# One hybrid encoder layer on one core: the feed-forward norm by way of memory, and the second stage's products and merges in another order

## The chip, the cores and the metric

The kernel runs on one core of one Trainium2 chip. The metric is the time of one execution in microseconds of device time (us). A core has five engines that work side by side and wait for each other through semaphores: PE (TensorE, matrix products; PEld is its loading of weights), DVE (VectorE), ACT (ScalarE), POOL (GpSimd) and SP (SyncE, which here only issues DMA transfers). Each engine takes its instructions strictly in the order of its own queue, so an instruction that waits holds back all that stand behind it.

## What is computed

One layer over 1024 frames of width 1024, in float32:

```python
u = rms_norm(h, mix_norm_gain)
proj = u @ w_in                  # attention and delta-rule inputs
o_att = band attention of 8 heads;  o_dn = gated delta rule of 4 heads
h = h + concat([rms_norm(o_att), o_dn]) @ w_out
z = rms_norm(h, ffn_norm_gain) @ w_ff1        # 1024 -> 4096
h = h + square(relu(z)) @ w_ff2               # 4096 -> 1024
```

The change concerns the first instructions, the step `h + ... @ w_out`, and the two feed-forward products.

## The kernel before

Activations lie transposed: features on the 128 partitions, frames along the free axis, in two halves of 512 frames. A float32 product is made of three fp32r matmuls: each operand is split into a high part (a cast, mostly on ACT) and a low part (operand minus high part, mostly on DVE), in `split`, and the products high·high, low·high and high·low are summed. A tile name ends in `_h` or `_l` accordingly.

The order of the instructions on each engine is made at compile time by a scheduler from the order of the code; nothing is reordered while it runs. `tc.issue_after(x)` asks it to place what follows behind the instruction `x`.

**Start.** For each of eight blocks k the kernel loads 128 rows of `w_in` (tile `wdk_r`, by `load_w`) and a block of x (tile `xt`, by `load_xt`), splits the weights (`wdk_h`, `wdk_l`), scales x by the norm's gain `mgain` (`uh` on ACT, `ul` on DVE) and squares it (`xs`). The first product of the kernel, `dk_ps` at L299, needs `uh` and `wdk_h` of block 0.

**Output projection (`out_proj`).** It makes h in four quarters, `rows(j, hf)`: j is the half of the features and hf the half of the frames. Each quarter is four 128x512 results `op`; after each, DVE adds x (L948, tile `h`), ACT squares it (L954) and POOL adds the square to the sum `op_q` (L955). Each quarter of h goes to memory (`h_dr`, L956), and after that ACT multiplies it by the gain of the second norm (L958). After both quarters of a half, `norm(hf, acc)` sums over partitions with a float32 matmul by a matrix of ones (tile `hs`, L963), takes 1/(mean+eps) with two DVE instructions (L964, L965) and writes that to memory (`r2_dr`, L966). `ff1` reads it back as `r2`. Since relu(r·z)² is r²·relu(z)², the norm's factor is applied after the square (`emit`, L1057).

**First feed-forward product (`ff1`).** Eight blocks of 512 columns of `w_ff1`. In each block a 2x2 blocking of the product is done with seven products instead of eight, `q1` to `q7`, whose operands are quarters or sums of quarters of the weights (`wa`, `ws`) and of h (`b11`, `b21`, `t1`, `t2`, `b22`, `t3`, `t4`; these are made once, by `uop`, in place in the quarters of h, and kept). A product is 24 matmuls of 128x512 into one of four PSUM buffers. Blocks 0 and 1 are interleaved at first: q1 of both, q2 of both, then the rest of each block. The results go to memory as `f_dr`.

**Second feed-forward product (`ff2`).** Four blocks of 1024 rows of `w_ff2`, again seven products `p1` to `p7` of 48 matmuls each, into two PSUM buffers. In block 0 the results of p1, p5, p6 and p7 are copied to `y` by ACT, the others are added by DVE. Block 3 (`last`) also merges the seven sums into the four quarters of the output and stores them; `p4` comes last, one PSUM buffer after the other, and is subtracted and stored in four pieces (L1252, L1253).

## Time and profile before

| | |
|---|---|
| time, median of 3 runs | 1311.7 us (1311.33 to 1311.72) |
| the profiled execution | 1309.98 us, of it the span 1307.9 us |
| busy: PE, DVE, ACT, POOL | 1265.2, 936.2, 553.0, 301.8 us |
| mean granted clock of TensorE | 0.988 of full speed |
| `out_proj` ends, `ff1` starts | about 673 us |
| `ff2` starts | about 990 us |
| last matmul starts | 1300.6 us |

The span is the time from the first to the last record of the profile. A busy share of 97% for PE says that nearly every microsecond of the span has a matmul in flight; it doesn't say at which clock. All times below are from the span's start.

### The profile page before, as it was taken

The page shows a single profiled execution, that of the slowest core. Times are in us where ns is not written, and L with a number is a line of the kernel's source. Part 1 is how long each engine was busy: PE and PEld are TensorE (multiplying, and loading weights), DVE is VectorE, ACT ScalarE, POOL GpSimd, SP SyncE. Part 2 cuts the span into 40 slices and gives each one's busy share as a digit, 9 for nine tenths or more (in the row PEclk, how much of TensorE's full clock was granted, in tenths as well). Part 3 has the DMA queues.
Part 4 walks back from the last instruction along what each step waited for, and adds up shares of the span by engine and source line. Part 5 has one row for each costly group of instructions (what it writes and reads, how often), then busy time and mean ns, then how long its engine had stood idle before and what let it go on. Part 6 is the DMA issues. An engine that isn't in the chain of part 4 may idle for free.

```text
span 1307.9 us, 17991 instructions
## 1 busy us (share of the span) xinstructions
PE 1265.2 (97%) x6658; PEld 1041.5 (80%) x6658; DVE 936.2 (72%) x1395; ACT 553.0 (42%) x918; POOL 301.8 (23%) x507
## 2 busy tenths in 40 slices
PE   8999999999999998979998999999998999999997
PEld 6778878788888777858776888888887888888886
DVE  7899978554056565853639756776669897897997
ACT  7233232233266563754335444444456443333330
POOL 4426552543033364533310000000000000000034
PEclk9999999999999999989998999999999999999999
DMA  7214254665573532114341323323379523322002
GB/s 219 70 45 142 94 157 123 137 161 155 193 225 111 153 94 74 56 46 165 117 153 61 111 100 121 104 92 102 109 249 353 169 86 113 129 82 97 15 33 96
DMA packets 129255, 160.63 MB, mean 123 GB/s; under 512 B 22800, under 2 KB 71952, under 8 KB 128656
## 3 DMA queue, kind: packets, MB, share of 16 engines
q1 hardware_dynamic: 111760, 138.51, 34.1%
q10 hardware_dynamic: 17408, 20.98, 4.7%
q8 instruction: 52, 0.85, 0.3%
q14 instruction: 35, 0.29, 0.1%
HBM read 111.75 MB, written 47.71 MB: 122 GB/s over the span
## 4 chain that ended last, share of the span: by engine, by line
PE 82%; DVE 10%; DMA 3%; issue 2%; POOL 1%; ACT 1%; POOLq 1%; SPq 0%; ACTq 0%; DVEq 0%
PE q L1051 21%; PE p L1128 20%; PE op L163 5%; PE av_ps L163 3%; PE aq_ps L163 3%; PE dk_ps L299 3%; PE t_o L851 3%; PE g_ps L163 3%; PE ak_ps L163 2%; PE dv_ps L163 2%; PE dq_ps L163 2%; PE t_tpb L830 1%; PE t_tpa L841 1%; PE t_sb L778 1%; DMA t_q<-q_dr 1%
## 5 line engine op out<-in xcount | busy, mean ns | idle before, releaser
L1197 POOL TENSOR_TENSOR y<-y,y 128x1024 f32<-128x1024 f32 x6 | 19.4, 3250 | 600.5 <-DVE y L1193 581.6
L794 DVE CUSTOM_DVE_ANT_0 t_pb<-t_sb,biasn 128x256 f32<-128x256 f32 (+1 forms) x64 | 25.7, 403 | 56.8 <-PE t_sb L779 31.2
L1193 DVE TENSOR_TENSOR y<-y,p 128x1024 f32<-128x1024 f32 x46 | 55.3, 1219 | 6.3 <-PE p L1128 5.4
L163 PE MATMUL op<-mh,wo_h 128*128 128x512 f32 x128 | 50.3, 393 | 0.6 <-ACT wo_h L142 0.3
L163 PE MATMUL op<-ml,wo_h 128*128 128x512 f32 x128 | 50.5, 394 | 0.0
L163 PE MATMUL op<-mh,wo_l 128*128 128x512 f32 x128 | 48.3, 391 | 0.0
L809 ACT ACTIVATE t_pb<-t_pb,t_nm 128x256 f32<-128x256 f32 (+1 forms) x64 | 31.7, 495 | 23.1 <-DVE t_nm L803 15.0
L948 DVE TENSOR_TENSOR h<-op,op_x 128x512 f32<-128x512 f32 x16 | 10.8, 688 | 29.7 <-PE op L163 29.7
L851 PE MATMUL t_o<-t_ta,vt 128*64 128x128 f32 x240 | 29.7, 299 | 1.8 <-DVE t_ta L844 1.1
L955 POOL TENSOR_TENSOR op_q<-op_q 128x512 f32<-128x512 f32 x14 | 19.6, 1399 | 48.2 <-ACT op_q L954 48.0
L803 DVE CUSTOM_DVE_ANT_0 t_pa<-t_sa,biaso,t_nm 128x384 f32<-128x384 f32 (+2 forms) x48 | 26.3, 549 | 5.5 <-PE t_sa L779 3.3
L163 PEld LDWEIGHTS op<-mh,wo_h 128*128 128x128 f32 x128 | 24.0, 188 | 6.8 <-ACT wo_h L142 0.7
L163 PEld LDWEIGHTS op<-mh,wo_l 128*128 128x128 f32 x128 | 24.0, 188 | 5.4 <-issue 0.4
L163 PEld LDWEIGHTS op<-ml,wo_h 128*128 128x128 f32 x128 | 24.0, 188 | 5.1 <-issue 0.2
L299 PE MATMUL dk_ps<-uh,wdk_h 128*128 128x512 f32 x56 | 21.7, 413 | 5.5 <-ACT uh L180 5.5
L778 PE MATMUL t_sb<-ks,t_q 128*128 128x256 f32 (+1 forms) x72 | 23.2, 333 | 3.7 <-DMA t_q<-q_dr 3.7
L812 ACT ACTIVATE t_pa<-t_pa,t_nm 128x384 f32<-128x384 f32 (+2 forms) x48 | 26.5, 552 | 0.1
L841 PE MATMUL t_tpa<-ident,t_pa 128*128 128x128 f32 x120 | 21.9, 288 | 4.5 <-ACT t_on L879 3.3
L163 PE MATMUL g_ps<-uh,wg_l 128*128 128x512 f32 x64 | 25.3, 398 | 0.5 <-POOL wg_l L145 0.5
L163 PE MATMUL dv_ps<-ul,wdv_h 128*128 128x512 f32 x64 | 25.5, 398 | 0.0
L851 PEld LDWEIGHTS t_o<-t_ta,vt 128*64 128x64 f32 x240 | 17.9, 143 | 9.5 <-issue 1.9
L163 PE MATMUL dq_ps<-uh,wdq_h 128*128 128x512 f32 x64 | 25.4, 396 | 0.0
(1101 smaller groups left out, 4429.7 us busy)
## 6 DMA issues: line engine op xcount, KB each, us to landing
wa<-in_w_ff_dram SPq DMA_DIRECT2D x32, 512.0 KB
a<-in_w_ff_dram SPq DMA_DIRECT2D x32, 512.0 KB
b<-f_dr SPq DMA_DIRECT2D x32, 512.0 KB
t_q<-q_dr SPq DMA_DIRECT2D x32, 256.0 KB
f_dr<-yy ACTq DMA_DIRECT2D x16, 512.0 KB
f_dr<-zz ACTq DMA_DIRECT2D x12, 512.0 KB
xt<-in_x_t_dram SPq DMA_DIRECT2D x16, 256.0 KB
ks<-k_dr SPq DMA_DIRECT2D x16, 256.0 KB
```

Of the source, the lines that this page charges most:

```text
L163: nc.tensor.matmul(ps, a, b, start=(i == 0), stop=(i == n - 1))
L299: nc.tensor.matmul(ps[ct], a[:, s], b, start=(k + m == 0), stop=(k == NKT - 1 and m == 2))
L778: nc.tensor.matmul(o, q[:, i * P:(i + 1) * P], k[:, c], start=True, stop=False)
L794: nc.vector.tensor_tensor_reduce(sb[:, c], bk[:, c], new[g][pp][:, c], -1.0, 3.0e38, ALU.add, ALU.min, nm[:, 4 + i:5 + i])
L803: nc.vector.tensor_tensor_reduce(sa[e][:, 0:wa], bk[:, 0:wa], old[g][i][:, 384 - wa:384], -1.0, nm[:, 4 + i:5 + i], ALU.add, ALU.min, nm[: ...
L809: nc.scalar.activation(sb[:, c], sb[:, c], AF.Exp, bias=m, scale=-1.0, accum_out=T["sums"][:, 4 + i:5 + i])
L812: nc.scalar.activation(sa[e][:, 0:wa], sa[e][:, 0:wa], AF.Exp, bias=m, scale=-1.0, accum_out=T["sums"][:, i:i + 1])
L841: nc.tensor.transpose(tp[:, js], sa[e][:, js], ident)
L851: nc.tensor.matmul(po[64 * e:64 * e + 64, pp * P:(pp + 1) * P], vt[k0 + j][:, 64 * h:64 * h + 64], (ta[e] if j < na else tb)[:, c:c + P], ...
L1051: nc.tensor.matmul(part(ps, q), l[:, s], r, start=(k + m == 0), stop=(k == 3 and m == 2))
L1128: nc.tensor.matmul(part(ps[q // 2], q % 2), l[:, s], part(r, k), start=(i + k + m == 0), stop=(i + k + m == 4))
L1193: nc.vector.tensor_tensor(y[i][m], y[i][m], ps[m], op)
```

## The change

1. At the start the matrix of ones is made first, and eight float32 128x128 matmuls on it, whose result nobody reads, are put at the head of PE's queue. The first block of x is loaded from ACT's queue instead of SP's, and on SP `mgain` comes first and the weights of block 0 after it.
2. `norm` is gone. `out_proj` writes the two sums of squares to memory (`sq_dr`), and `ff1` reads both back as one tile `acc`. `norm_col`, called when q1 of blocks 0 and 1 is issued, sums over partitions with eight float32 matmuls of one column each (`hcol`) and takes 1/(mean+eps) of a 128x8 tile (`r_col`). `norm_row`, called after the q2s, spreads it with eight float32 128x128 matmuls (`hrow`), and ACT copies the result to `r2`.
3. `square` (relu and square) is taken out of `emit` and comes ahead of it. In blocks 0 and 1 the generator yields between the two.
4. `LAST` orders the splits of the operands b22, t3 and t4 behind the first split of t1, t2 and b22.
5. `ff2` makes its products in the order p1, p2, p5, p3, p6, p7, p4 instead of p1, p5, p2, p3, p6, p7, p4, with the loads in step.
6. In the last block `y6 += y1` moves from DVE to POOL and comes early, `y7 += y6` and `y3 += y6` come before p6 is added, and p6 and p7 are then added straight to the outputs (y3 and y7; y4 and y5). Two of the last four stores go to ACT's queue.

```diff
+WARM = 8
+LAST = {"b22": "t1", "t3": "t2", "t4": "b22"}
...
+    ones = cpool.tile([P, P], F32, name="ones")
+    nc.gpsimd.memset(ones, 1.0)
+    warm = bank(ps_o, "warm")
+    for i in range(WARM):
+        nc.tensor.matmul(warm[:, 0:P], ones, ones, start=True, stop=True)
     ident = cpool.tile([P, P], F32, name="ident")
...
-        nc.sync.dma_start(out=raw, in_=x_t[k, :, hf * TH:(hf + 1) * TH])
         if not hf and not k:
+            nc.scalar.dma_start(out=raw, in_=x_t[0, :, 0:TH])
             nc.sync.dma_start(out=mgain, in_=mix_gain)
+        else:
+            nc.sync.dma_start(out=raw, in_=x_t[k, :, hf * TH:(hf + 1) * TH])
...
     for k in range(NKT):
-        w_dk.append(load_w(w_in[k * P:(k + 1) * P, DK:DK + 512], f"wdk_{k}"))
+        if k:
+            w_dk.append(load_w(w_in[k * P:(k + 1) * P, DK:DK + 512], f"wdk_{k}"))
         load_xt(0, k)
+        if not k:
+            w_dk.append(load_w(w_in[0:P, DK:DK + 512], "wdk_0"))
...
         acc = rows(1, 0, acc)
-        norm(0, acc)
+        nc.sync.dma_start(out=sq_dr[:, 0:TH], in_=acc)
         mixed(1)
         acc = rows(1, 1, None)
         acc = rows(0, 1, acc)
-        norm(1, acc)
+        nc.sync.dma_start(out=sq_dr[:, TH:SEQ], in_=acc)
...
+        def norm_col():
+
+            acc = page2("ut4", "acc")
+            nc.sync.dma_start(out=acc, in_=sq_dr)
+            ps = psw.tile([P, 1024], F32, tag="bk", name="hcol")
+            for q in range(NT):
+                nc.tensor.matmul(ps[:, q:q + 1], acc[:, q * P:(q + 1) * P], ones[:, 0:1], start=True, stop=True)
+            nc.vector.tensor_scalar(r_col, ps[:, 0:NT], 1.0 / DM, EPS, ALU.mult, ALU.add)
+            nc.vector.reciprocal(r_col, r_col)
+
+        def norm_row():
+
+            ps = psw.tile([P, 1024], F32, tag="bk", name="hrow")
+            for q in range(NT):
+                nc.tensor.matmul(ps[:, q * P:(q + 1) * P], r_col[:, q:q + 1].broadcast_to([P, P]), ident,
+                                 start=True, stop=True)
+            nc.scalar.copy(r2.rearrange("p a t -> p (a t)"), ps)
...
-                bop = uop(key)
+                ah, al = parts(src, n + "a", key)
+                if key in LAST:
+                    hi, lo = begun[LAST[key]]
+                    with tc.issue_after(hi), tc.issue_after(lo):
+                        bop = uop(key)
+                else:
+                    bop = uop(key)
...
-        for _ in range(2):
+        for i in range(2):
             for g in first:
                 next(g)
+            (norm_row if i else norm_col)()
...
             accumulate(1, product(f"p1{kb}", lambda i: (a11[i], b11[i])))
-            accumulate(5, product(f"p5{kb}", prep5))
             accumulate(2, product(f"p2{kb}", lambda i: (a12[i], b21[i])))
             if last:
                 merge(nc.gpsimd, 2, 1)
                 store(y[2], 0, 0)
-            accumulate(3, product(f"p3{kb}", prep3))
-            accumulate(6, product(f"p6{kb}", prep6))
+                merge(nc.gpsimd, 6, 1)
+            accumulate(5, product(f"p5{kb}", prep5))
             if last:
-                merge(nc.vector, 6, 1)
                 merge(nc.gpsimd, 3, 5)
                 for m in range(2):
                     nc.gpsimd.tensor_tensor(y[5][m], y[5][m], h11[m], ALU.add)
-                merge(nc.vector, 3, 6)
-                store(y[3], 0, 1)
-            accumulate(7, product(f"p7{kb}", prep7))
+            accumulate(3, product(f"p3{kb}", prep3))
+            ps = product(f"p6{kb}", prep6)
             if last:
                 merge(nc.vector, 7, 6)
+                merge(nc.vector, 3, 6)
+                accumulate(3, ps)
+                store(y[3], 0, 1)
+                accumulate(7, ps)
+                merge(nc.vector, 4, 7)
                 merge(nc.gpsimd, 5, 7)
-                merge(nc.vector, 4, 7)
+            else:
+                accumulate(6, ps)
+            ps = product(f"p7{kb}", prep7)
+            if last:
+                accumulate(4, ps)
+                accumulate(5, ps)
                 store(y[5], 1, 1)
+            else:
+                accumulate(7, ps)
...
-                nc.sync.dma_start(out=out[0, (4 + q) * P:(5 + q) * P, 0:TH], in_=t)
+                (nc.scalar if q % 2 else nc.sync).dma_start(out=out[0, (4 + q) * P:(5 + q) * P, 0:TH], in_=t)
```

What the scheduler makes of it is seen at three places. In the rows, a number behind a name tells apart tiles of one name. First, ACT's queue at the start of the program, before:

```order
L142 ACT_TABLE_LOAD
L142 CAST wdk_h<-wdk_r 128x512
L185 ACTIVATE xs_176<-xt_171 128x512
L180 ACTIVATE uh_0_141<-xt_171,mgain 128x512
L142 CAST wdk_h<-wdk_r 128x512
L180 ACTIVATE uh_1_143<-xt_184,mgain 128x512
```

and now:

```order
L179 DMA xt_174<-in_x_t_dram 128x512
L184 ACT_TABLE_LOAD
L184 ACTIVATE uh_0_150<-xt_174,mgain 128x512
L189 ACTIVATE xs_179<-xt_174 128x512
L146 CAST wdk_h<-wdk_r 128x512 x2
L184 ACTIVATE uh_1_152<-xt_193,mgain 128x512
L189 ACTIVATE xs_197<-xt_193 128x512
```

The load of ACT's function table stood ahead of all waits and now stands behind the x transfer, in front of the first instruction that reads `mgain`; the cast of the first weights has moved from the first to the third place.

Second, DVE's queue at the start of `ff1`. Before, from the two instructions of `norm(1, acc)` on (`op_q` is the sum of squares, the `h` are quarters of h that become t1 and t3 in place, `t1h`/`t1l` their parts):

```order
L964 TENSOR_SCALAR op_q<-hs_7328 128x512
L145 TENSOR_TENSOR b22l_7650<-h_7069,b22h_7649 128x1024
L965 RECIPROCAL op_q<-op_q 128x512
L145 TENSOR_TENSOR b22l_7654<-h_7069,b22h_7653 128x1024
L1018 TENSOR_TENSOR h_6731<-h_7198,h_6731 128x1024 x2
L1075 TENSOR_TENSOR ws_0_7559<-wa_0_7555,wa_0_7557 128x1024
L1018 TENSOR_TENSOR h_7198<-h_7069,h_7198 128x1024 x2
L145 TENSOR_TENSOR t1l_7568<-h_6731,t1h_7567 128x1024
```

and now, from the low part of t1 up to the reciprocal of the norm:

```order
L147 TENSOR_TENSOR t1l_7589<-h_6740,t1h_7588 128x1024
L147 TENSOR_TENSOR q_0a_l<-ws_0_7580,q_0a_h 128x1024
L147 TENSOR_TENSOR b22l_7671<-h_7074,b22h_7670 128x1024
L1018 TENSOR_TENSOR h_6740<-h_7074,h_6740 128x1024
L147 TENSOR_TENSOR t1l_7594<-h_6740,t1h_7593 128x1024
L1104 TENSOR_TENSOR ws_0_7580<-ws_0_7580,wa_0_7399 128x1024
L147 TENSOR_TENSOR b22l_7675<-h_7074,b22h_7674 128x1024
L1032 TENSOR_SCALAR r_col<-hcol 128x8
L147 TENSOR_TENSOR t2l_7630<-h_6740,t2h_7629 128x1024
L1018 TENSOR_TENSOR h_6740<-h_7074,h_6740 128x1024
L1108 TENSOR_TENSOR wa_0_7401<-wa_0_7401,ws_0_7580 128x1024
L1033 RECIPROCAL r_col<-r_col 128x8
```

The reciprocal of 128x512 has gone; that of 128x8 stands eleven rows further on than this piece begins, behind the low parts of t1, q5 and b22 and the subtractions that make t2.

Third, ACT's queue where `ff2` starts (the y copies take the results of p1, the `p50` and `p20` tiles are operands of p5 and p2 in block 0). Before:

```order
L1191 COPY y_9450<-p_9496 128x1024
L142 CAST p50b_h<-b_0_9462 128x1024
L142 CAST p50a_h<-s_0_9601 128x1024
L1191 COPY y_9450<-p_9497 128x1024
L142 CAST p50b_h<-b_0_9464 128x1024
L142 CAST p20a_h<-a_0_9478 128x1024
L1058 DMA f_dr<-yy_9174 128x2x512
L142 CAST p20b_h<-b_0_9482 128x1024
```

and now:

```order
L1221 COPY y_9473<-p_9519 128x1024
L146 CAST p50b_h<-b_0_9485 128x1024
L146 CAST p50a_h<-s_0_9692 128x1024
L1221 COPY y_9473<-p_9520 128x1024
L146 CAST p50b_h<-b_0_9487 128x1024
L1083 DMA f_dr<-yy_9197 128x2x512
L146 CAST p20a_h<-a_0_9489 128x1024
L146 CAST p20b_h<-b_0_9493 128x1024
```

The casts of the operands of p2 still stand behind the copies and the casts for p5, while on PE the first two matmuls of p2, which read `p20a_h` and `p20b_h`, now stand directly behind p1 and ahead of all of p5.

## Rows read from the trace of the kernel before

**Rows 1.** The page: busy time, share of the span and instructions of PE and of its weight loads.

```profile
PE 1265.2 (97%) x6658; PEld 1041.5 (80%) x6658; DVE 936.2 (72%) x1395; ACT 553.0 (42%) x918; POOL 301.8 (23%) x507
```

**Rows 2.** Waits of PE over the whole span: what it waited for, us in total, how often, the longest.

```profile
PE dk_ps L299 <- ACT uh L180: 5.5, 1, 5.5
PE hs L963 <- POOL op_q L955: 2.9, 1, 2.9
PE p L1128 <- DVE p50b_l L145: 2.9, 1, 2.9
PE q L1051 <- DVE z L1057: 2.9, 1, 2.9
```

**Rows 3.** Windows: from:to in us, its length, then for each engine the busy us and the number of instructions, the granted clock of PE (1.00 is full speed, 0.50 half), the share of the DMA engines and GB/s.

```profile
498.00:499.00 1.00, 1.00 (x5) 1.00 (x6) 0.00 (x0) 0.00 (x0) 0.00 (x0) 0.55 0.00 0
1000.00:1020.00 20.00, 16.40 (x65) 12.74 (x64) 20.00 (x19) 11.35 (x12) 0.00 (x0) 0.91 0.76 275
1007.00:1010.00 3.00, 3.00 (x9) 2.32 (x8) 3.00 (x3) 1.65 (x2) 0.00 (x0) 0.50 1.00 336
```

**Rows 4.** Timeline of PE within the mixers. Timeline rows give start in us, duration in us, engine, line, operation, output and inputs, and how many records are drawn together; in brackets the idle time before and what ended it.

```profile
497.92 1.94 PE L453 MATMUL c_po<-c_vn,c_att 128*128 128x128 f32 x8 [2.01 <-POOL c_att L655]
```

**Rows 5.** Timeline of the first 14 us, SP's issues (SPq), ACT and PE.

```profile
0.79 0.39 SPq L151 DMA_DIRECT2D wdk_r<-in_w_in_dram  x1
0.79 1.28 ACT L142 ACT_TABLE_LOAD   x1 [0.79 <-PEq L1336]
3.54 0.62 ACT L142 CAST wdk_h<-wdk_r 128x512 fp32r<-128x512 f32 x1 [1.46 <-DMA wdk_r<-in_w_in_dram]
4.21 0.63 ACT L185 ACTIVATE xs<-xt 128x512 f32<-128x512 f32 x1
4.74 0.71 ACT L180 ACTIVATE uh<-xt,mgain 128x512 fp32r<-128x512 f32 x1
5.50 2.08 PE L299 MATMUL dk_ps<-uh,wdk_h 128*128 128x512 f32 x4 [5.50 <-ACT uh L180]
7.80 0.63 PE L299 MATMUL dk_ps<-uh,wdk_l 128*128 128x512 f32 x1
8.23 0.63 PE L299 MATMUL dk_ps<-ul,wdk_h 128*128 128x512 f32 x1
10.20 0.40 PE L299 MATMUL dk_ps<-uh,wdk_l 128*128 128x512 f32 x1
```

**Rows 6.** Timeline of PE: float32 matmuls of one column (eight of them) and of 128 columns (four of them) in the mixers; a float32 matmul shows as two records.

```profile
29.48 1.84 PE L246 MATMUL rcol<-ones,xs 128*128 128x1 f32 x16
37.90 1.16 PE L251 MATMUL rrow<-ident,r_col 128*128 128x128 f32 x8
```

**Rows 7.** Timeline of PE: the first `hs` (one float32 matmul of 512 columns) within the output projection.

```profile
636.45 1.02 PE L963 MATMUL hs<-op_q,ones 128*128 128x512 f32 x2
```

**Rows 8.** Timelines from the end of the output projection to the end of q7 of block 0: DVE, SP, POOL, ACT, SP, two DVE subtractions in a row, and PE with ten matmuls from the first row to the last.

```profile
673.00 0.69 DVE L948 TENSOR_TENSOR h<-op,op_x 128x512 f32<-128x512 f32 x1 [4.80 <-PE op L163]
673.72 0.34 SPq L956 DMA_DIRECT2D h_dr<-h  x1
674.56 1.26 POOL L955 TENSOR_TENSOR op_q<-op_q 128x512 f32<-128x512 f32 x1 [4.21 <-ACT op_q L954]
679.25 2.57 ACT L958 ACTIVATE h<-h,fgain 128x512 f32<-128x512 f32 x4 [1.53 <-DMA h_dr<-h]
683.10 0.34 SPq L966 DMA_DIRECT2D r_dr<-op_q  x1
685.14 0.34 SPq L993 DMA_DIRECT2D r<-r_dr  x1
690.87 1.22 DVE L1087 TENSOR_TENSOR wa<-wa,wa 128x1024 f32<-128x1024 f32 x1
692.00 1.22 DVE L145 TENSOR_TENSOR q_1a_l<-wa,q_1a_h 128x1024 fp32r<-128x1024 f32 x1
727.22 0.39 PE L1051 MATMUL q<-t3h,q_0a_h 128*128 128x512 f32 x1
729.26 0.39 PE L1051 MATMUL q<-t4h,q_0a_h 128*128 128x512 f32 x1
```

**Rows 9.** Timelines of ACT and PE where p1 of block 0 in `ff2` ends: the copy of p1's first buffer, p1's last matmul, the cast `p20b_h`, and the matmul that ends the second wait of PE.

```profile
1000.10 1.02 ACT L1191 COPY y<-p 128x1024 f32<-128x1024 f32 x1 [2.98 <-PE p L1128]
1001.03 0.39 PE L1128 MATMUL p<-p10b_h,p10a_l 128*128 128x512 f32 x1
1005.70 1.06 ACT L142 CAST p20b_h<-b 128x1024 fp32r<-128x1024 f32 x1
1005.75 0.50 PE L1128 MATMUL p<-p50b_l,p50a_h 128*128 128x512 f32 x1 [2.91 <-DVE p50b_l L145]
```

**Rows 10.** The end: a store of y on SP, DVE's last two subtractions, SP's last issue, and two windows.

```profile
1300.04 0.37 SPq L1153 DMA_DIRECT2D out_dram<-y  x1
1300.99 1.28 DVE L1252 TENSOR_TENSOR y<-y,p 128x512 f32<-128x512 f32 x2 [2.04 <-PE p L1128]
1303.39 1.14 SPq L1253 DMA_DIRECT2D out_dram<-y  x1
1300.00:1301.00 1.00, 0.95 (x5) 0.45 (x3) 0.01 (x1) 0.00 (x0) 1.00 (x2) 1.00 0.05 20
1306.00:1307.00 1.00, 0.00 (x0) 0.00 (x0) 0.00 (x0) 0.00 (x0) 0.00 (x0) 0.50 0.45 170
```

More of the change, by code (lines that the diff above doesn't have):

```diff
@@ L107, in hymba_kernel @@
     tri_s = mpool.tile([P, P], F32, name="tri_s")
-    ones = cpool.tile([P, P], F32, name="ones")
-    nc.gpsimd.memset(ones, 1.0)
     for t, pat, cm, base in ((tri_u, 1, -1, 0), (tri_s, -1, 1, -1)):
@@ L140, in split @@
     def split(src, hi, lo, hi_eng, lo_eng):
-        if hi_eng is nc.scalar:
-            nc.scalar.copy(hi, src)
-        else:
-            hi_eng.tensor_copy(hi, src)
-        lo_eng.tensor_tensor(lo, src, hi.bitcast(F32), ALU.subtract)
+        a = nc.scalar.copy(hi, src) if hi_eng is nc.scalar else hi_eng.tensor_copy(hi, src)
+        return a.ins, lo_eng.tensor_tensor(lo, src, hi.bitcast(F32), ALU.subtract).ins
     lo_turn = [0]
@@ L236, in hymba_kernel @@
     f_dr = dram.tile([DFF // P, P, SEQ], F32, name="f_dr")
-    r2_dr = dram.tile([P, SEQ], F32, name="r2_dr")
+    sq_dr = dram.tile([P, SEQ], F32, name="sq_dr")
     mix = [[None, None], [None, None]]
@@ L959, in rows @@
             return acc
-        def norm(hf, acc):
-            ps = bank(ps_o, f"hs{hf}")
-            nc.tensor.matmul(ps, ones, acc, start=True, stop=True)
-            nc.vector.tensor_scalar(acc, ps, 1.0 / DM, EPS, ALU.mult, ALU.add)
-            nc.vector.reciprocal(acc, acc)
-            nc.sync.dma_start(out=r2_dr[:, hf * TH:(hf + 1) * TH], in_=acc)
         weights(0)
@@ L992, in ff1 @@
         r2 = pools["r2"][0].tile([P, 2, TH], F32, tag="r2", name="r2", bufs=1)
-        nc.sync.dma_start(out=r2, in_=r2_dr.rearrange("p (a t) -> p a t", a=2))
+        begun = {}
         def page2(tag, name, dt=F32):
@@ L997, in page2, with parts @@
             return pool.tile([P, 1024], dt, tag=tag, name=name, bufs=n)
-        def parts(src, name):
+        def parts(src, name, key):
             count[0] += 1
@@ L1003, in parts @@
             lo = page2("l2" if late else "l", name + "_l", F32R)
-            split(src, hi, lo, nc.scalar, nc.vector)
+            begun.setdefault(key, split(src, hi, lo, nc.scalar, nc.vector))
             return hi, lo
@@ L1043, in product @@
                 ps = psw.tile([P, 1024], F32, tag="bk", name=n)
-                ah, al = parts(src, n + "a")
-                bop = uop(key)
+                ah, al = parts(src, n + "a", key)
[5 more added lines that the diff above has]
+                    bop = uop(key)
                 for k in range(4):
@@ L1052, in product, with square, emit @@
                 return ps
-            def emit(t, fh, th):
+            def square(t):
                 nc.scalar.activation(t, t, AF.Relu)
                 nc.scalar.activation(t, t, AF.Square)
+            def emit(t, fh, th):
                 nc.vector.tensor_tensor(two(t), two(t), r2[:, th:th + 1, :].broadcast_to([P, 2, TH]), ALU.mult)
@@ L1069, in block @@
             nc.vector.tensor_tensor(z11, y1, ps, ALU.add)
+            square(z11)
+            yield
             emit(z11, 0, 0)
-            yield
             if sb <= 1:
@@ L1085, in block @@
             nc.vector.tensor_tensor(z12, y5, ps, ALU.add)
+            square(z12)
             emit(z12, 0, 1)
@@ L1090, in block @@
             nc.vector.tensor_tensor(y5, y5, ps, ALU.add)
+            square(y5)
             emit(y5, 1, 1)
@@ L1093, in block @@
             nc.vector.tensor_tensor(y1, y1, ps, ALU.subtract)
+            square(y1)
             emit(y1, 1, 0)
         first = [block(sb) for sb in range(2)]
-        for _ in range(2):
+        for i in range(2):
             for g in first:
                 next(g)
+            (norm_row if i else norm_col)()
         for g in first + [block(sb) for sb in range(2, DFF // FB)]:
@@ L1174, in ff2 @@
             a11, b11 = wq("r", "a11", k1, 0), fq("r", "b11", k1, 0)
+            a12, b21 = wq("r2", "a12", k2, 0), fq("r2", "b21", k2, 0)
             a21, a22, b12 = wq("rc", "a21", k1, 1), wq("rc", "a22", k2, 1), fq("rc", "b12", k1, 1)
-            a12, b21 = wq("r2", "a12", k2, 0), fq("r2", "b21", k2, 0)
             b22 = fq("r2", "b22", k2, 1)
```

## The prediction

> **What bounds the kernel now.** I read the page first: PE is busy for 1265.2 us, 97% of the span [rows 1], and the chain of work that ended last runs through PE for most of its length. So a term counts only where PE stands still, runs at the lower of its two clocks, or has something removed or added. The waits of PE come next [rows 2]: besides the start (5.5 us) three single waits of 2.9 us stand in the stages that the change touches: one for the sum of squares ahead of `hs`, one in `ff1`, one in `ff2`. The windows show what follows such a wait [rows 3]: from 1007 to 1010 the granted clock is 0.50, that is 1.2 instead of 2.4 GHz, and the 20 us from 1000 on hold 65 matmuls, where ten matmuls in a dense stretch take from 727.22 to 729.26 [rows 8], 0.227 us each. At the lower clock one takes 0.43 us, as from 7.80 to 8.23 [rows 5]. The reader should keep both: a wait costs its own length, and then about 0.2 us for each matmul until the clock is back. DVE's share in `ff1` and at the start of `ff2` matters as a queue: PE's waits there are for the tail of that queue.
>
> I sum against the profiled execution (span 1307.9, time 1309.98 us); the median of the runs is 1.7 us above it.
>
> **Start.** The first product waits for one chain on ACT. Now the chain is: `mgain` lands, function table, `uh`, `xs`, `wdk_h`. `mgain` is issued first; the nearest transfer, the weights issued at 0.79, was there at 3.54 [rows 5], which is my value for `mgain`; it is the upper end for a smaller transfer. The lower end is the other write of this kernel whose landing shows, 2.0 us (683.10 to 685.14, [rows 8]). Then 1.28 for the table, which before lay under the wait for the weights, 0.71, 0.53 (4.21 to 4.74) and 0.62: 6.7, with the lower end 6.0, against 5.50. So the product starts 0.5 to 1.2 us later. Against that stand the eight warm-up matmuls. Before, PE worked for 4.7 us (5.50 to 10.20) until the rhythm went over to 0.23, eleven matmuls that cost 0.2 us too much each, 2.2 us. The warm-ups are 128 columns wide in float32; four such took 1.16 us [rows 6], so eight take 2.3 us at the high clock and 4.6 at the low one, from some 1 us on (my estimate: once the matrix of ones is made). That ends 1 to 3 us ahead of the first product and is no longer than what the clock needed before, so the outcome is open: I take half, -1.1, and +1.1 for the later start. Term 0, ends -1.7 and +1.2. The Trainium skill, page "TensorE: Matmul & The Clock Gate", Part 1 (The HAM clock gate), says that the throttled clock is the default state and that activity releases it; by that rule alone the eleven matmuls would run at full speed and the term would be -1.1. The wait of 2.01 us in [rows 4], after which the clock fell [rows 3], is why I don't take it whole.
>
> **Output projection.** The first `hs` took 1.02 us in the midst of dense matmuls [rows 7]: -1.0. The other lies in the next term. The four DVE instructions that go lie under PE's work.
>
> **Start of `ff1`.** From DVE's last addition of h, which ends at 673.69, to the matmul after q7 of block 0 at 729.26 [rows 8] PE needed 55.6 us. Now, on the same clock: q1 of block 0 needs the PSUM buffer that this addition frees, so it starts at 673.75. Two q1s are 48 matmuls, 10.9 us, to 684.65. `hcol` then needs `acc`. Its chain: POOL's last addition ends at 675.82; the write is issued behind `h_dr` on SP. It lands 2.0 us later at best (683.10 to 685.14) and 5.5 us later at worst (`h_dr`, four times the bytes, 673.72 to 679.25). I take 5.5, since `h_dr` and weight loads are ahead of it: 681.4. The read back is two times those bytes: between 2.0 and 5.5, I take 3.5 because the loads are through by then. So `acc` is there at 685 (ends 680 and 687): PE waits 0.4 us (0 to 2.3). While `acc` is waited for nothing of the two norms moves on PE, and q2 stands behind it. Then `hcol` 1.84 us, as the eight matmuls of one column [rows 6], to 686.85, and two q2s, to 697.8.
>
> `hrow` needs the reciprocal on DVE, and that stands far back. The subtraction that makes t1 needs two of ACT's four multiplications by the gain. These began at 679.25 and took 2.57 us [rows 8]; now a cast for q2 that needs q1's end and the copy of q1 stand ahead of them, so the second ends at 682.3. From there fourteen 1024-wide instructions up to the reciprocal at 1.13 us (690.87 to 692.00) are 15.8 us, and the two small ones some 0.3: 698.5. PE waits 0.7 us for it, hidden if `acc` was late. `hrow` is twice the four matmuls of 1.16 us: 2.3, to 700.8. q5, q6, q3 and q7 are 96 matmuls, 21.8 us, to 722.6. Their low parts stand behind the reciprocal in the order of use, each product gives DVE 5.4 us, and the two later splits that LAST holds back no longer stand ahead of them. So q7 ends 6.6 us earlier: -6.6. Ends: `acc` at 687 gives -5.5, no wait at all -7.8.
>
> The Trainium skill, page "DMA: Bandwidth & Descriptors", section "Anatomy of one DMA", gives a DMA about 2 us fixed, mostly for confirming the last byte, plus bytes at 436 GB/s; my estimate by that is 2.6 and 3.2 us for the two trips, `acc` at 681.7, and no wait. `h_dr` at 5.5 us [rows 8] is where the trace differs from it. The sum by that rule would be 0.4 better at most.
>
> **Steady state of `ff1` and `ff2`.** The same operations in nearly the same order, with PE dense over them: nothing. It is covered by DVE's free share there, and if that cover went, each late low part would cost its own lateness.
>
> **Start of `ff2`.** p1 ends at 1001.03 + 0.23. Before, PE then waited 0.7 us, ran two matmuls of p5, and waited 2.9 us for `p50b_l` until 1005.75 [rows 2, 9]. Now p2's first two matmuls stand ahead of p5, and they need `p20b_h`. On ACT that cast still stands behind the copies of p1, the first of which begins at 1000.10 when p1's first buffer is done; it ran from 1005.70 to 1006.76 [rows 9]. All behind p1 on PE waits for it: 5.5 us. By then p5's low parts are done, so no second wait follows. PE resumes at 1006.76, having done nothing, where before it resumed at 1005.75 with two matmuls done: +1.5. Afterwards the clock falls as before; before it lost some 1.5 us (half speed from 1007 to 1010, [rows 3]), after a longer wait I take 0.6 more, up to the 2.2 of the start. Term +2.1, ends +1.0 and +2.5.
>
> **The end.** Before, POOL's last merge delayed the store of y5, and the last two pieces were issued behind it on SP, the last from 1303.39 to 1304.53; data flowed until about 1306.45 (share 0.45 of that window), 1.45 us ahead of the span's end [rows 10]. Now y5 needs p7 only, whose end is 10.9 us ahead of the last matmul, so its stores are through. DVE's last subtraction ends at 1302.27 as before; the last piece goes out on ACT at once. Its bytes start some 0.9 us after issue (store at 1300.04, first bytes in the last 5% of that window), 256 KB take 0.7 us at 170 GB/s over a share of 0.45, and 1.45 us follow: 1305.3. Term -2.5; ends -1.5 if earlier stores still stand ahead, -3.0.
>
> **Sum.** 0 - 1.0 - 6.6 + 2.1 - 2.5 = -8.0: span 1299.9, profiled execution 1302.0, median 1303.7 us.
>
> **Rivals.**
> - The clock also falls in `ff1`. For: after a wait of 2.01 us in the mixers [rows 4] the clock was 0.55 in 498 to 499 [rows 3]; q1, `hcol` and `hrow` each have a short wait ahead now, and `hcol` has one column per matmul. Against: none of my waits there is above 1 us. Price 1.5 to 2.2 us: 1305.2 to 1305.9, up to 1307 with a late `acc`. The skill's page on TensorE, Part 1, names idleness as what throttles the array, which is on the side of this rival. Chance 0.15.
> - The warm-ups work whole and p2's casts are no later than p5's low part was: -1.1 and -1.5 to -2: about 1301, down to 1299.5. Against it stands ACT's order. Chance 0.15.
> - The change doesn't do what it says: DVE is as full as before, so that low parts of q3 or q7 are late as now, 2.9 us and 14 matmuls at the low clock, 2.8 us: 1309.4. For: the same fourteen instructions and all of t3 and b22 remain. Against: two reciprocals and the early splits are gone from ahead. Chance 0.10.
> - Slower: `acc` comes so late that all of PE stands at `hcol`. Each us behind 685 costs one. My gain is used up when it lands at 693, slower by 0.2% at 695.7, that is 20 us after POOL's sum, against 5.5 for the slowest trip shown. Then 1314.3 or more. Chance 0.05.
> - My forecast, 1301.5 to 1305: 0.55.
>
> **How the numbers follow.** 0.2%, 2.6 us, is about what a measurement can tell from no change. Faster than 1309.1: the forecast, the first two rivals and a part of the third, 0.87; the rest of the third is the same, 0.08; slower 0.05. The range reaches from the second rival to the third, 1299.5 to 1309.0.
>
> **What would show it.** In the profile after: the wait ahead of `hs` gone, waits ahead of `hcol` and `hrow` below 1 us each and a clock of 1.00 from 680 to 720; the reciprocal of `r_col` near 698; no wait for q3; one wait of about 5.5 us behind p1 in `ff2`, for `p20b_h`, and half speed after it; first product near 6.5 us; data of the stores ending 1.5 us after DVE's last subtraction. Wrong it would be if `hcol` waits several us, if the `ff2` wait isn't there, or if DVE falls behind in q5 to q7.

## The result, and the profile after

The changed kernel is slower, by little: the ratio of its runs to those of the kernel before is 1.003, 95% interval 1.0016 to 1.0045, medians 1316.3 us (20 runs) against 1312.5 us (20 runs). The forecast was 8 us faster. The profiled execution took 1311.28 us (span 1309.2), the shortest of its twenty and 5 us below their median; the profiled one of before took 1309.98. In the mixers, between 440 and 600 us, the granted clock falls in other places from one execution to the next (440 to 460 us: 0.91 before, 1.00 after, 0.91 in e1, 0.83 in e11; 540 to 560: 0.99, 0.94, 1.00, 1.00), so an absolute time late in a trace carries that with it. I therefore compare four stretches that begin and end with the same work: from the last matmul of the output projection to the first of p1 of block 0 (`ff1`), from there to the first of p1 of block 3 (`ff2`, three blocks), from there to the last matmul (the last block), and from there to the end of the span.

| us | `ff1` | `ff2`, blocks 0 to 2 | last block | end |
|---|---|---|---|---|
| before | 317.8 | 234.3 | 75.9 | 7.4 |
| after | 313.7 | 236.4 | **84.3** | 4.9 |
| difference | -4.1 | +2.1 | **+8.4** | -2.5 |

The sum is +3.9 us, and the medians are 3.8 apart (the interval reaches from 2.1 to 5.9). That the two agree so closely is in part luck, since `ff1` differs between executions of the same program: 313.7 to 315.8 us in the six traces of this study that have the changed one, mean 314.7, and 316.6 to 317.8 in the three that have the old one, mean 317.4. By these means `ff1` gains 2.7 us, not 4.1. The last block doesn't move like that: 75.9 us in every trace in which PE has no wait there. Two of the four stretches are as predicted, one is smaller, and one, the last block, had no term at all.

The same views as ahead of the prediction, now of the changed kernel. The page's row of busy times, against [rows 1]:

```profile
PE 1267.2 (97%) x6702; PEld 1044.5 (80%) x6702; DVE 937.3 (72%) x1395; ACT 554.3 (42%) x919; POOL 306.0 (23%) x509
```

The waits of PE (what it waited for, us in total, times, longest), against [rows 2]:

```profile
PE p L1158 <- ACT p20b_h L146: 5.4, 1, 5.4
...
PE p L1158 <- DVE p43b_l L147: 2.5, 1, 2.5
PE hcol L1031 <- DMA acc<-sq_dr: 2.2, 1, 2.2
...
PE p L1158 <- DVE y L1223: 2.0, 1, 2.0
...
PE dk_ps L306 <- ACT wdk_h L146: 1.5, 1, 1.5
```

The waits for `hs`, for `z` and the 5.5 us at the start are gone. `p20b_h` was foretold. `hcol` waits longer than foretold, and the two waits for `p43b_l` and `y`, both in the last block, are new.

Windows of the last block (from:to, length, then busy us and instructions of PE, PEld, DVE, ACT and POOL, the granted clock, DMA share, GB/s), of after; the first is the whole block:

```profile
1220.01:1304.34 84.33, 79.80 (x336) 65.07 (x335) 78.57 (x56) 21.91 (x22) 31.40 (x10) 0.96 0.11 44
...
1260.00:1265.00 5.00, 4.30 (x12) 3.44 (x13) 5.00 (x4) 0.10 (x1) 4.28 (x2) 0.66 0.01 3
...
1295.00:1300.00 5.00, 5.00 (x16) 3.94 (x15) 5.00 (x5) 0.00 (x0) 0.00 (x0) 0.66 0.22 88
```

The last block of before:

```profile
1224.63:1300.57 75.94, 75.94 (x337) 62.90 (x335) 70.94 (x54) 22.08 (x22) 24.27 (x8) 1.00 0.07 28
```

The products need 75.9 us. DVE is busy for 78.6 us now: it has become the bound of this block, and PE waits for it twice and runs at the low clock after each wait (12 and 16 matmuls in 5 us, where 22 fit; 0.7 us of the first window still belong to the wait). The two waits are 4.5 of the 8.4 us; the rest goes with the low clock behind them. But DVE has only two instructions more, 2.3 us, and is busy for 7.6 us more. The timelines of DVE (first fence) and POOL (second) show why:

```profile
1259.43 1.21 DVE L1223 TENSOR_TENSOR y<-y,p 128x1024 f32<-128x1024 f32 x1
1260.56 1.21 DVE L147 TENSOR_TENSOR p33b_l<-b,p33b_h 128x1024 fp32r<-128x1024 f32 x1
1261.70 1.21 DVE L1223 TENSOR_TENSOR y<-y,p 128x1024 f32<-128x1024 f32 x1
1262.83 2.26 DVE L147 TENSOR_TENSOR p63a_l<-s,p63a_h 128x1024 fp32r<-128x1024 f32 x1
1265.02 3.42 DVE L147 TENSOR_TENSOR p63b_l<-b,p63b_h 128x1024 fp32r<-128x1024 f32 x1
1268.36 3.42 DVE L147 TENSOR_TENSOR p73a_l<-a,p73a_h 128x1024 fp32r<-128x1024 f32 x1
1271.70 3.42 DVE L147 TENSOR_TENSOR p73b_l<-b,p73b_h 128x1024 fp32r<-128x1024 f32 x1
...
1290.02 3.38 DVE L147 TENSOR_TENSOR p43b_l<-b,p43b_h 128x1024 fp32r<-128x1024 f32 x1
```

```profile
1260.72 6.63 POOL L1227 TENSOR_TENSOR y<-y,y 128x1024 f32<-128x1024 f32 x2 [5.70 <-DVE y L1223]
1267.31 6.72 POOL L1265 TENSOR_TENSOR y<-y,h 128x1024 f32<-128x1024 f32 x2
...
1286.60 5.72 POOL L1227 TENSOR_TENSOR y<-y,y 128x1024 f32<-128x1024 f32 x2 [12.56 <-DVE y L1223]
```

A 1024-wide DVE instruction takes 1.21 us, and 3.4 us while POOL adds two tiles of y. The addition of a PSUM tile (`y<-y,p` at 1261.70) stays at 1.21 beside a POOL addition; the ones that read both operands from SBUF don't, unless they began first, as `p33b_l` did at 1260.56. The operand for which PE waits, `p43b_l`, is itself one of the long ones. The chain that ended last runs through DVE here until PE takes over (start, us, what):

```profile
1265.09 3.21 DVE p63b_l L147
...
1284.19 4.53 DVE y L1223 x4
1288.72 1.38 DVE p43a_l L147
1290.09 3.32 DVE p43b_l L147
1293.45 11.29 PE p L1158 x41
```

This reading is what the first experiments test: it could also be the order of the products, or simply the additions that stand ahead of operands on DVE.

The start of `ff1` after, against [rows 8]: SP's write and read, `hcol` and the first `hrow` records on PE, the reciprocal on DVE, and the window behind `hcol`:

```profile
673.36 0.97 SPq L978 DMA_DIRECT2D sq_dr<-op_q  x1
...
681.18 0.34 SPq L1028 DMA_DIRECT2D acc<-sq_dr  x1
```

```profile
684.51 1.92 PE L1031 MATMUL hcol<-ones,acc 128*128 128x1 f32 x16 [2.21 <-DMA acc<-sq_dr]
...
698.94 1.27 PE L1039 MATMUL hrow<-ident,r_col 128*128 128x128 f32 x10
```

```profile
695.87 0.20 DVE L1033 RECIPROCAL r_col<-r_col 128x8 f32<-128x8 f32 x1
```

```profile
687.00:691.00 4.00, 4.00 (x12) 3.08 (x12) 4.00 (x4) 1.18 (x2) 0.00 (x0) 0.57 0.00 0
```

The read is issued 7.8 us after the write, and `hcol` starts 3.3 us after that. PE waits 2.2 us, and from 687 to 691, behind the wait and `hcol`, the clock is 0.57: 12 matmuls where 17 or 18 fit. `hrow` waits for nothing.

The start of `ff2`, against [rows 9]:

```profile
1000.06 1.22 PE L1158 MATMUL p<-p20b_h,p20a_h 128*128 128x512 f32 x2 [5.38 <-ACT p20b_h L146]
```

### The profile page after: what moved, and what is told of

It reads as the page before. It is cut to its first block, busy times and chain, and to the rows that moved or that the text cites. A ratio compares the mean times of both kernels' runs of the same rounds, so it can differ in the third digit from the quotient of the medians.

```text
span 1309.2 us, 18076 instructions
## 1 busy us (share of the span) xinstructions
PE 1267.2 (97%) x6702; PEld 1044.5 (80%) x6702; DVE 937.3 (72%) x1395; ACT 554.3 (42%) x919; POOL 306.0 (23%) x509
## 4 chain that ended last, share of the span: by engine, by line
PE 73%; DVE 8%; DMA 3%; ACT 2%; POOL 1%; issue 1%; SPq 0%; DVEq 0%; ACTq 0%; POOLq 0%
PE q L1074 23%; PE p L1158 19%; PE op L165 5%; PE av_ps L165 3%; PE aq_ps L165 3%; PE t_o L858 3%; PE g_ps L165 3%; PE ak_ps L165 2%; DVE y L1223 1%; PE t_tpb L837 1%; PE t_tpa L848 1%; PE t_sb L785 1%; PE t_sa L785 1%; DMA t_q<-q_dr 1%; PE t_sb L786 1%
## 5 line engine op out<-in xcount | busy, mean ns | idle before, releaser
L1227 POOL TENSOR_TENSOR y<-y,y 128x1024 f32<-128x1024 f32 x8 | 24.7, 3111 | 587.7 <-DVE y L1223 587.7
L1223 DVE TENSOR_TENSOR y<-y,p 128x1024 f32<-128x1024 f32 x50 | 59.9, 1216 | 5.3 <-PE p L1158 4.4
L165 PE MATMUL g_ps<-uh,wg_h 128*128 128x512 f32 x64 | 25.2, 394 | 1.2 <-ACT wg_h L146 1.2
L165 PE MATMUL dv_ps<-uh,wdv_l 128*128 128x512 f32 x64 | 25.4, 397 | 0.0
L165 PE MATMUL aq_ps<-waq_h,uh 128*128 128x512 f32 x64 | 25.3, 401 | 0.0
```

Source lines behind the costliest of these rows:

```text
L165: nc.tensor.matmul(ps, a, b, start=(i == 0), stop=(i == n - 1))
L1223: nc.vector.tensor_tensor(y[i][m], y[i][m], ps[m], op)
L1227: eng.tensor_tensor(y[i][m], y[i][m], y[z][m], ALU.add)
```

## The experiments

All ratios are to the kernel before, the experiments' from five rounds each; differences to the changed kernel are differences of these ratios, times 1312 us. A ratio is good to about 2 us (that of e6 to 3) and a difference of two ratios to about 3, so what is smaller than that rests on the traces. The four stretches of the table above, for every kernel run (us, from its profiled execution):

| kernel | ratio (95% interval) | `ff1` | `ff2`, 0 to 2 | last block | end |
|---|---|---|---|---|---|
| changed kernel | 1.0030 (1.0016, 1.0045) | 313.7 | 236.4 | 84.3 | 4.9 |
| e1, merges as before | 0.9979 (0.9961, 0.9996) | 315.4 | 236.3 | 75.9 | 6.7 |
| e2, product order as before | 1.0019 (1.0005, 1.0034) | 315.6 | 235.2 | 82.9 | 4.9 |
| e3, whole second stage as before | 0.9959 (0.9941, 0.9977) | 313.9 | 235.3 | 75.9 | 6.7 |
| e4, start alone | 0.9983 (0.9965, 1.0000) | 317.8 | 234.3 | 75.9 | 7.4 |
| e5, additions on VectorE | 0.9964 (0.9945, 0.9983) | 315.8 | 236.1 | 75.9 | 5.2 |
| e6, `hcol` behind both q2 | 1.0074 (1.0050, 1.0099) | 319.5 | 236.0 | 84.3 | 4.9 |
| e7, e2 + e5 + e6 | 0.9995 (0.9974, 1.0016) | 319.5 | 235.0 | 75.9 | 4.8 |
| e8, e5 + e6 | 1.0005 (0.9990, 1.0020) | 319.6 | 236.1 | 75.9 | 5.2 |
| e9, e10 + `hcol` between the q2s | 0.9949 (0.9932, 0.9967) | 311.8 | 234.0 | 75.9 | 4.9 |
| e10, e2 + e5 | 0.9975 (0.9959, 0.9991) | 313.9 | 235.3 | 75.9 | 4.9 |
| e11, before, additions on VectorE | 0.9979 (0.9960, 0.9998) | 316.6 | 234.3 | 75.9 | 4.8 |

**e1: the last block's additions back in their places, the products' order new.**

```diff
             if last:
                 merge(nc.gpsimd, 2, 1)
                 store(y[2], 0, 0)
-                merge(nc.gpsimd, 6, 1)
             accumulate(5, product(f"p5{kb}", prep5))
+            accumulate(3, product(f"p3{kb}", prep3))
+            accumulate(6, product(f"p6{kb}", prep6))
...
```

What is left out is the rest of the additions, in the order and on the engines of the kernel before.

> The changed kernel, with the additions to the sums of the second stage's last block put back to the places and engines they had before; its order of products stays the new one. Theory A (the last block's additions, ten instead of eight on GpSimd and two more on VectorE, are what holds its products up by the 8.4 us by which it is longer): about 8 us less than the changed kernel, that is about 1303 us by its profiled 1311.3, and PE's waits of 1.99 us at p63 and 2.55 us at p43b_l are gone or below 0.5 us each. Theory B (the order of the products, p2 ahead of p5 and the loads of a12 and b21 ahead of a21, is what costs in the last block): no change within 1.5 us, the two waits stay.

Measured: 6.7 us less than the changed kernel; PE has no wait in the last block, which takes 75.9 us again. Theory A holds, B is out: the order of the products costs nothing in the last block.

**e2: the order of before, the additions as changed.** The four lines of the loads and products in their old order.

> The changed kernel with the order of the products and loads of the second stage as before (p1, p5, p2), its additions in the last block as changed. Theory A (the additions hold the last block up): only the later start of the second stage is undone, 2 us less than the changed kernel, about 1309 us, and the last block stays some 8 us longer than before. Theory B (the order does): 10 us less, about 1301 us.

Measured: 1.4 us less than the changed kernel, which the noise doesn't tell from the 2 expected or from nothing; the last block stays at 82.9 us, with waits of 3.7 us for `p43b_l` and 0.9 us for `p63b_l`. This is theory A again, from the other side.

**e3: the whole second stage as before,** two queues for the last stores kept.

> The changed kernel with the whole second stage (order of products and loads, additions of the last block) as before, but the last stores still on two queues. By the ledger of the two traces (start of the second stage 2.0 us later, last block 8.4 us longer) theories A and B both say about 10.5 us less than the changed kernel, 1301 us, so some 9 us below the kernel before. Theory C (what the first stages gain is handed back in the second stage whatever its order, since it waits for loads or clock): no more than 3 us below the kernel before.

Measured: 9.3 us less than the changed kernel and 5.4 below before, where 9 were expected. Of that, its trace shows 4.0 in `ff1` and 0.6 at the end, and it loses 1.0 in `ff2`. Theory C is out, by the trace above all: the interval of the ratio reaches from 3.0 to 7.7 us below before, and the theory allowed 3. The expectation was too high since it counted on the whole of the short end, which the old merges don't give (6.7 us, not 4.9).

**e4: the start alone.**

> The kernel before with the change to its first 10 us alone (eight matmuls that warm the clock, the first loads on two queues, mgain ahead of the weights). By the ledger its first products start 1.5 us earlier at full clock and nothing later answers: 1.5 us below the kernel before (1.0 to 2.0), which five rounds can just tell from nothing. Rival (later waits take it back, as those at the norms of the first feed-forward stage): within 0.5 us of the kernel before.

Measured: ratio 0.9983, with an interval that reaches to 1. By the trace the start gains nothing: the last `dk_ps`, the eighth block's, starts at 55.94 us, at 56.03 before and at 56.26 in the changed kernel. And the expectation had taken one execution for the rule. The first matmuls of e4 (first fence) don't come in the rhythm of those of the changed kernel's trace (second fence):

```profile
6.97 0.63 PE L308 MATMUL dk_ps<-ul,wdk_h 128*128 128x512 f32 x1
7.40 0.63 PE L308 MATMUL dk_ps<-uh,wdk_h 128*128 128x512 f32 x1
```

```profile
6.65 0.39 PE L306 MATMUL dk_ps<-ul,wdk_h 128*128 128x512 f32 x1
6.88 0.39 PE L306 MATMUL dk_ps<-uh,wdk_h 128*128 128x512 f32 x1
```

Eleven of the traces have the warm-up matmuls. In three of them (the changed kernel, e6 and e9) the first products run at 0.23 us a matmul, in the other eight at 0.43. All are level at 56 us, the three too; where these give their lead back I did not locate.

**e5: the same additions, in the same places, on VectorE.** This tells A1 from A2.

```diff
-                merge(nc.gpsimd, 6, 1)
+                merge(nc.vector, 6, 1)
...
```

The merges (2, 1), (3, 5) and (5, 7) and the addition of `h11` to y5 change in the same way.

> The changed kernel with the ten additions of the last block that it gives to GpSimd done by VectorE instead, in the same places of the program; nothing else differs. Theory A1 (a GpSimd addition slows the VectorE operations that run beside it, from 1.21 us each to some 3.4 us; the 26.9 us of stretch on VectorE between 1224 and 1306 us in the changed kernel are this): VectorE takes on ten additions of 1.21 us, 12.1 us, and loses about 26 us of stretch, so the last block falls back from 84.3 us to the 75.9 us of its products; the short end (4.9 us behind the last product) stays: about 8.4 us less than the changed kernel, 1303 us by its profiled 1311.3. Theory A2 (it is the count of additions ahead of the products' operands on VectorE that holds them up, not GpSimd): VectorE has still more ahead of them, and the last block gets longer than 84.3 us by up to 12 us.

Measured: 8.7 us less than the changed kernel. The window of the whole last block:

```profile
1225.79:1301.72 75.93, 75.93 (x336) 62.90 (x335) 73.03 (x66) 22.03 (x22) 0.00 (x0) 1.00 0.10 37
```

DVE has ten instructions more than in the changed kernel's window (66 and 56) and is busy 5.5 us less. Per instruction that is 1.11 us; 56 would be 62 us, so the ten additions on POOL had cost DVE 16.6 us (an estimate from these means), 1.7 us each, where DVE does one itself in 1.1. The expectation had put this at 26 us. A1 holds, A2 is out.

**e11: the same in the kernel before.**

> The kernel before with the eight additions of its last block that stand on GpSimd done by VectorE, nothing else. Theory A1 (a GpSimd pair costs VectorE 4.4 us, done by VectorE 2.3): its products are not held up before or after, so only the end behind the last product can shrink, from 7.3 us to about 5: 1.5 to 2.5 us less, just to be told from nothing. Theory A2 (additions on VectorE hold up the products' operands): more than 2 us longer.

Measured: ratio 0.9979, 2.8 us. The last block takes 75.9 us as before, and the end shrinks from 7.4 to 4.8 us. So the shorter end of the changed kernel needs neither the second queue nor other merges: it comes when POOL's last, late addition is gone. e1 and e3, which keep it and have two queues for the last stores, gain 0.6 us of the 2.5.

**e6: `hcol` two products later, `hrow` one.** This is on the other miss, the start of `ff1`.

```diff
-        for i in range(2):
+        for _ in range(2):
             for g in first:
                 next(g)
-            (norm_row if i else norm_col)()
+        norm_col()
+        next(first[0])
+        norm_row()
```

The added `next` issues q5 of block 0. What is left out: in blocks 0 and 1 `emit` comes behind that, in e9 behind q6.

> The changed kernel with the small products that sum the squares (hcol) two products later, behind both q2, and the ones that spread the result (hrow) behind q5_0, the first two blocks' z11 being scaled after that. Theory D (in the first feed-forward stage TensorE loses 2.2 to 2.5 us waiting for the sums of squares to come back from memory, and then 2 to 4 us at half clock): both are gone, 4 to 6 us less than the changed kernel. Rival (the wait only moves, to the sums' next reader or to the scaled z11 and its buffers): the 2 us of the wait come back elsewhere, less than 1.5 us gained.

Measured: 5.8 us more than the changed kernel; a miss. The wait at `hcol` is gone, and a longer one stands at `hrow`. PE's rows and DVE's:

```profile
698.86 1.84 PE L1031 MATMUL hcol<-ones,acc 128*128 128x1 f32 x16
713.40 2.90 PE L1039 MATMUL hrow<-ident,r_col 128*128 128x128 f32 x12 [7.09 <-DVE r_col L1033]
```

```profile
708.45 0.16 DVE L1032 TENSOR_SCALAR r_col<-hcol 128x8 f32<-128x8 f32 x1
713.06 0.19 DVE L1033 RECIPROCAL r_col<-r_col 128x8 f32<-128x8 f32 x1
```

`hcol` ends at 700.70. The two small DVE instructions that follow need 0.35 us of work, but their places in DVE's full queue are 7.8 and 12.4 us behind it. The rival's form was right, its size was not: not 2 us came back but 7.1 and the low clock after it (0.76 in the 12 us from 713 on).

**e7 and e8: all edits together, with the old and the new order.**

> The changed kernel with three edits together: the order of the second stage's products and loads as before, the last block's additions as changed but all on VectorE, and hcol and hrow later as in the run on that alone. If the three costs add (8.4 us for the additions, 1 to 2 us for the start of the second stage, 4 to 6 us at hcol), 13 to 16 us less than the changed kernel: ratio to the kernel before 0.990 to 0.993, 1299 to 1302 us. If the gain in one place is handed back in the next (clock, loads), less than 9 us below the changed kernel, no better than the run with the second stage as before (ratio 0.996).

> As the run with all three edits, but with the changed kernel's order of products and loads in the second stage. By the traces (first product to block 1's first product: 84.0 us with the new order, 82.9 with the old) it should be 1 to 2 us above that run: ratio to the kernel before 0.991 to 0.995. If the order's loss belongs to that execution's clock, the same within 0.5 us.

Measured: 0.9995 and 1.0005. Both carry the 7.1 us at `hrow`, as e6 does, so e7's sum is missed for that reason; the last block is at 75.9 us in both. The old order is worth 1.3 us by these two ratios, less than their intervals, and 1.1 us by their traces; by the ratios of e5 and e10, which differ in the order alone, it costs 1.4. What it is worth therefore rests on the traces.

**e9 and e10: `hcol` only one product later and `hrow` far enough behind it, beside the same kernel without that.** e10 is e2 with all additions on VectorE; e9 adds:

```diff
-        for i in range(2):
-            for g in first:
-                next(g)
-            (norm_row if i else norm_col)()
+        for g in first:
+            next(g)
+        next(first[0])
+        norm_col()
+        next(first[1])
+        next(first[0])
+        norm_row()
```

The three added `next` issue q2 of block 0, q2 of block 1, and q5 and q6 of block 0.

> The changed kernel with the second stage's order of products and loads as before and the last block's additions as changed but on VectorE; start and first feed-forward stage as changed. The run with the whole second stage as before had the ratio 0.996 and 6.7 us behind its last product, the one with the additions on VectorE 5.3: so 1.5 to 2 us less than the former, ratio 0.994 to 0.995 to the kernel before. Theory A2, that more additions on VectorE hold the products up: ratio 0.998 or more.

> The run beside it (second stage's order as before, the last block's additions on VectorE) with hcol one product later, between the first two blocks' q2, and hrow behind block 0's q6. In the run that put hcol behind both q2 the wait for the load was gone, but the scaling and the reciprocal of r_col stood in VectorE's queue and ended 12 us behind hcol, so hrow, asked for after one more product, waited 7.1 us. Here VectorE reaches the reciprocal some 4 instructions of 1.14 us after its place in the changed kernel (695.9 us), about 701 us on that kernel's clock, and TensorE has work until 706. Theory D (the wait at hcol and the clock behind it cost 4 to 6 us): 4 to 6 us less than the run beside it. Rival (what goes there comes back, at hrow or at the scaled z11): within 1.5 us of it.

Measured: e10 0.9975, a miss: 0.994 to 0.995 was expected. Theory A2, which asked for 0.998 or more, isn't the reason: the last block takes 75.9 us and PE waits for nothing in it. Where the ratio loses against those of e3 and e5 stays open. e9 0.9949: 3.4 us less than e10, 6.7 us below the kernel before, the lowest ratio of this study, though its interval overlaps those of e3 and e5. PE's rows of e9 and its window from 680 to 720:

```profile
688.48 1.84 PE L1031 MATMUL hcol<-ones,acc 128*128 128x1 f32 x16
...
706.65 1.95 PE L1039 MATMUL hrow<-ident,r_col 128*128 128x128 f32 x16
```

```profile
680.00:720.00 40.00, 40.00 (x194) 33.48 (x192) 39.20 (x37) 24.45 (x27) 0.00 (x0) 1.00 0.24 81
```

Neither waits, and the clock stays at 1.00. In the changed kernel this window has 176 matmuls, a busy PE of 37.79 us and a clock of 0.96. From the last matmul of the output projection to the first after q7 of block 0 e9 takes 48.5 us and e10 52.8: 4.3 us, the expected size; the five other traces of the changed stage have 52.6 to 54.7 us there. 1.5 us of it go back soon after to two waits of block 1 for its operands (0.6 us for `q_1a_l`, 0.9 us for `q_1a_h`), 0.7 us more I did not locate, and `ff1` as a whole is 2.1 us shorter. Theory D is right in its mechanism; the gain in time, 3.4 us, is below the 4 to 6 expected, by less than its noise.

## Why the prediction failed, step by step

- **Steady state and last block, "nothing": the step that failed.** I put the whole of `ff2` behind its start at nothing, with DVE's free share as the cover, and never costed edit 6, the last block's merges: two instructions more on DVE and two more on POOL. They cost 8.4 us, and e1 and e5 show where: POOL's additions lengthen DVE's instructions until DVE, not PE, sets the pace. The rows that would have told it were in the trace of before, DVE's (first fence) beside POOL's additions of 1268.35 and 1274.06, of which two single ones are shown (second fence):

```profile
1269.49 2.35 DVE L145 TENSOR_TENSOR p73a_l<-a,p73a_h 128x1024 fp32r<-128x1024 f32 x1
1271.77 3.41 DVE L145 TENSOR_TENSOR p73b_l<-b,p73b_h 128x1024 fp32r<-128x1024 f32 x1
1275.10 3.42 DVE L145 TENSOR_TENSOR p43a_l<-a,p43a_h 128x1024 fp32r<-128x1024 f32 x1
```

```profile
1268.35 2.42 POOL L1197 TENSOR_TENSOR y<-y,y 128x1024 f32<-128x1024 f32 x1 [5.12 <-issue]
1270.72 3.38 POOL L1197 TENSOR_TENSOR y<-y,y 128x1024 f32<-128x1024 f32 x1
```

  With them, and DVE busy for 70.9 of 75.9 us in that block, the sum is easy. Five us of slack; two more additions on DVE (2.3 us) and two more on POOL (up to 2.2 us each for DVE, 3.42 less 1.21): 6.7 us. DVE no longer fits, even before any wait lowers the clock. The cover that I named was DVE's free share, and the only share that I had read was the mean of the span, 72% [rows 1]; this stage has 93%. The Trainium skill, page "SBUF — State Buffer", section "SBUF: two separate sides", says it outright: VectorE instructions with two operands in SBUF and GpSimd instructions take turns at a shared pair of ports, and the other one is held up for the whole instruction. The trace agrees: POOL's two additions end at 1270.77 and 1274.10, and the two DVE instructions beside them 1.1 us behind each, at 1271.84 and 1275.18; POOL's second one takes 3.38 us where the first, with none of these ahead of it, took 2.42; and the addition with its operand in PSUM stays at 1.21 us.
- **Start of `ff1`, -6.6: a size too large.** From DVE's last addition of h (ends 671.02) to the matmul after q7 (722.52) it took 51.5 us, 4.1 less than before. Most single terms hold: q1 at 671.17, the reciprocal where foretold (698.5 on the clock of before, 695.8 with the whole stage 2.7 us earlier; measured 695.87), `hcol` 1.92 us, `hrow` 1.95, no wait for q3 or q7. What failed is the write of `acc`: I took the slowest trip shown, 5.5 us, as its upper end, and it was 7.8; the read back took 3.3 of the 3.5 foretold. The prediction's estimate by the Trainium skill, page "DMA: Bandwidth & Descriptors", section "Anatomy of one DMA", 2.6 us, fell further short for the write; that section is on transfers issued by GpSimd, and this one is issued by SP. So PE waited 2.2 us where I took 0.4 and gave 2.3 as the upper end, at which -5.5 would have been left. The clock then fell, the rival that I gave 0.15. The size hangs on the execution: the wait is 2.2 to 2.7 us in all six traces of the changed stage, and the stretch is 52.6 to 54.7 us by how long the clock stays low behind it (over the 12 us from the wait's end 0.86 in the changed kernel, 0.72 in e1). e9, without the wait, gets 4.3 us more than e10 at this place: the mechanism of the term was right.
- **Start of `ff2`, +2.1: right.** 5.38 us of waiting for `p20b_h`, then the low clock; +2.1 over blocks 0 to 2. All five traces with the new order have 236.0 to 236.4 us, those with the old one 234.0 to 235.3. The old order lost 1.0 us too in e2, e3 and e10 (235.2 to 235.3), 0.7 in e7, and nothing in e9 (234.0): behind the same wait of 2.9 us PE ran 37 matmuls in the next 10 us before, and 33 in e3. So by the traces the order is worth 0.7 to 2.4 us, and which it is hangs on how long the clock stays low.
- **The end, -2.5: right in size (-2.5),** for the reason that I gave first, POOL's last merge; e11 and e3 show that the second queue, which I used to work out the number, gives 0.6 of it.
- **The start, 0: right in size, with luck.** The first product starts at 6.32 us, near the 6.5 foretold, and in the profiled execution at the full rhythm of 0.23 us, so that the warm-ups worked whole there: at 16 us PE has done 43 matmuls, against 37 before. At 56 us both kernels are level, by something that no term of mine names. In eight of eleven traces the warm-ups didn't bring that rhythm (e4). The half that I took stood for an open outcome, and it was open. The measured ratio of e4 alone would leave a gain of 0 to 4.6 us.
- **The first `hs`, -1.0: open.** The output projection took 100.7 us before and 100.1 after, but 101.6 in e1, which is the same program there. Its executions differ by more than the term.

Of the rivals, "DVE is as full as before" fell (no wait for q3 or q7), "`acc` late" and "the clock falls in `ff1`" came true in part, of "the warm-ups work whole" the first half came true in that one execution and the second didn't (`p20b_h` was late), and the one that decided was not among them.

## What to carry to other kernels

Cost every instruction that an edit adds in the stage where it lands, with that stage's own share: a mean of 72% over the span hid 93% in the last block. An addition moved to GpSimd is not free for VectorE: here it took 1.4 to 1.7 us of VectorE's time on average, more than the 1.1 us in which VectorE does it. And a small result that goes through a full queue (the reciprocal of 128x8) arrives when the queue lets it: place its reader by that queue, not by the work.

## What the runs showed of the hardware that I had not expected

- A 128x1024 float32 addition on GpSimd with operands in SBUF takes 2.4 us (2.42 at 1268.35 before) and 3.4 us in turns with VectorE (3.38 at 1270.72); VectorE's 1.21 us instructions beside it take 3.4 us when both their operands lie in SBUF; the one with an operand in PSUM stayed at 1.21 us. In the last block before, 24.3 us of GpSimd cost VectorE 11.2 us (an estimate: 70.9 less 54 times 1.11).
- The write of 256 KB to memory with weight loads around it took 7.8 us from its issue to the issue of the dependent read, against 5.5 us for a write of four times the bytes before [rows 8]; in the ten kernels that have this write it took 7.8 to 8.1 us. A write of the same 256 KB in the kernel before took 2.0 us (683.10 to 685.14, [rows 8]). What makes the difference was not isolated.
- Eight float32 matmuls of 128 columns at the head of PE's queue, done 1.4 to 1.7 us ahead of the first product, were followed by matmuls at 0.23 us in three traces and at 0.43 us in eight.
- A wait of 2.2 us and eight matmuls of one column were followed by a granted clock of 0.57 over 4 us in the changed kernel, and in e1, after 2.3 us, of 0.72 over 12 us; e9, with the same eight matmuls and no wait, kept 1.00.
